# The ramp of a hybrid encoder layer: the w_ada sums of groups three and four at three places, with their block sums apart

## The chip, the cores and the metric

The kernel runs on one core of one Trainium2 chip. Its metric is the time of one execution in device microseconds (us). TensorE (PE in the profile) does the matrix products, VectorE (DVE) and ScalarE (ACT) the elementwise work, GpSimd (POOL) some memsets; the queue of SyncE (SP) issues nearly all DMA transfers. Each engine works through its own instructions in order and waits for others by semaphores.

## The reference, cut to what matters

```python
mod = jax.nn.silu(c) @ w_ada + b_ada                 # (1, 6144): shift, scale, gate
shift, scale, gate = jnp.split(mod, 3, axis=-1)
h = rmsnorm(x, pre_g) * (1.0 + scale[:, None]) + shift[:, None]
proj = h @ w_in                                      # (1024, 2048) @ (2048, 4608)
q, k, v, gate_a, u, gate_p = jnp.split(proj, SPLIT_POINTS, axis=-1)
y_a = windowed_gqa(q, k, v, rel_table, sink) * jax.nn.silu(gate_a)
y_p = multiscale_pool(u, w_pool_grp, pool_scale) * jax.nn.silu(gate_p)
g = jax.nn.sigmoid(h @ w_merge + b_merge)
g_a, g_p = jnp.split(g, N_BRANCHES, axis=-1)
merged = g_a * (y_a @ w_br_attn) + g_p * (y_p @ w_br_pool)
return x + gate[:, None] * rmsnorm(merged @ w_out, post_g)
```

Everything is float32; x is 1024 rows of 2048 columns. The change concerns only `silu(c) @ w_ada` for shift and scale, and the order in which weights arrive.

## The kernel before, in words

**Products.** The large products run by Strassen's scheme: seven products per 2 x 2 block step instead of eight, each on float32 values split into a high and a low part. `strassen` (L213) is a generator that yields after each of its seven products; `product` (L234) issues, for each, high x high, low x high and high x low. On PE a product's output bank is called X, V or Z. The seven in order are X (moving operand B11), V (T3), Z (T2), X again (B21), V again (T4), Z again (T1), and Z a last time (B22). `run` (L325) steps one generator for a pair of 128-column weight blocks; the seventh product of a run is put off (`late`) and issued by `flush` (L320) in the next run, after its second product.

For the weights, ACT writes the high part `whi` and DVE the low part `wlo` (both have four buffers) from the raw weights `raw` (four joint buffers), and DVE forms weight sums in `raw` and `ws`. After its second V product, DVE's addition `u<-V,u` empties bank V, and the next run's V product needs that bank.

**The ramp.** At the start, the normalized and modulated input h is not there yet; it is produced 512 columns at a time. w_ada's columns for shift and scale are taken in groups of 256 each. Group j of w_ada (16 tiles `ada`, one for each k block of 128 rows) gives the scale and shift for two k blocks of h. `modulation` (L476) makes four steps of four k blocks each: thin matmuls (GEMV, 32 columns wide, stationary operand `scz`, the silu of c) into one bank; after the fourth step ACT copies the bank to `acc`, `sum_columns` (L454) adds the four 32-row parts on PE (PM, the block sums), and `mod_columns` (L460) writes the columns `modc` on DVE. `fill` (L551) then modulates x, and makes the split operands B11 to B22 (the "op tiles") of one j with about a dozen instructions on each of ACT and DVE.

Groups one and two (j = 0, 1) are summed before the products. Five column pairs of w_in then run over the first half of k (j = 0, 1): pair one in plain blocks, pairs two to five as runs one to four of `ramp_gen` (L598). After these, the same five pairs run over the second half of k (j = 2, 3), which needs groups three and four. Their sums are issued between the products of runs one and two, by the table `late_sums` (L633): `run` calls one entry of `side` after each of its seven places, so entry 0 stands after run one's X, entry 6 after its last Z, entry 7 after run two's X; at a run's third place the put-off product of the run before is issued.

**What sets the order.** PE's order is that of the code; the instructions of `modulation` are pinned. ACT, DVE and SP are ordered by a scheduler from the same code, with pinned instructions (`keep`) in code order. On SP the w_ada tiles and raw weights are issued in the order of the code at L615 to L629; in the ramp SP has at most eight transfers under way, so a transfer is issued when an earlier one has landed. Raw weights of pair i are fetched by `fetch_raws` (L607); group four's tiles are ten in a pool of their own (`ada_tile`, L446) and six in slots of the large pool (`ada_slots`, L467).

Of the kernel before, what the change touches and what calls it, by code (L numbers as in the profile page):

```python
# [43 lines left out]
def encoder_layer(ctx: ExitStack, tc: tile.TileContext, x, c, table, w_ada, b_ada, pre_g,  # L44
# [32 lines left out]
    def uid(s):  # L77
        cnt[0] += 1
        return f"{s}_{cnt[0]}"

    def bank(tag, name="b"):
        return psum.tile([P, 512], F32, tag=tag, name=uid(name), bufs=1 if tag in SEEDED else 2)

    def slot(name, dt=F32R, shape=(P, 512)):
        return big.tile(list(shape), dt, tag="big", name=uid(name))

    def f32(ap):
        return ap.bitcast(F32)


    def keep(ins):

        tc.keep_in_program_order(ins)
# [31 lines left out]
    RAMP = 5  # L125
# [55 lines left out]
    def load_raws(w, n0, rows, js, pin=False):  # L181

        raws = []
        nj = len(js)
        joint = wp.tile([P, 2, nj, 256], F32, tag="raw", name=uid("raw"), bufs=4) if nj < 4 else None
        for kh in range(2):
            r = joint[:, kh] if nj < 4 else wp.tile([P, nj, 256], F32, tag="raw", name=uid("raw"), bufs=4)
            ins = load(r, rows(w, js, kh)[:, :, n0:n0 + 256])
            if pin:
                keep(ins)  # L190
            raws.append(r)
        return raws
# [6 lines left out]
    def rows_in_turn(part):  # L199

        def rows(w, js, kh):
            r0 = (part * 8 + 2 * js[0]) * P
            return w[r0:r0 + 2 * len(js) * P].rearrange("(k h p) n -> h p k n", h=2, p=P)[kh]
        return rows
# [135 lines left out]
    def weight_of(n0):  # L340
        return (w_in, n0) if n0 < NIN else (w_merge, n0 - NIN)
# [104 lines left out]
    def ada_tile(j, q):  # L446
        at = xa.tile([P, 2, 4, P], F32, tag="xa", name=uid("ada"))
        for kk in range(2):
            r0 = (2 * q + kk) * P
            keep(load(at[:, kk].rearrange("p (g h) n -> p g (h n)", g=2),  # L450
                      w_ada[r0:r0 + P, 0:2 * D].rearrange("p (g n) -> p g n", g=2)[:, :, j * 256:(j + 1) * 256]))
        return at

    def sum_columns(acc):  # L454
        pm = bank("at", "PM")
        for g in range(4):
            nc.tensor.matmul(pm[:, g:g + 1], acc[:, g, :], ones, start=True, stop=True)
        return pm

    def mod_columns(j, pm):  # L460
        tc.keep_in_program_order(nc.vector.tensor_tensor(
            modc[:, :, :, j], pm[:, 0:4].rearrange("p (g h) -> p g h", g=2),
            cols[:, 16:48].rearrange("p (g k) -> p g k", g=2)[:, :, 2 * j:2 * j + 2], ALU.add))
        keep(nc.vector.scalar_tensor_tensor(modc[:, 1, :, j], modc[:, 1, :, j], 1.0,
                                            cols[:, 48 + 2 * j:50 + 2 * j], op0=ALU.add, op1=ALU.mult))

    def ada_slots(j, kcs=range(KT)):  # L467
        tiles = []
        for kc in kcs:
            tiles.append(slot("ada", F32, (P, 4, P)))  # L470
            load(tiles[-1].rearrange("p (g h) n -> p g (h n)", g=2),
                 w_ada[kc * P:(kc + 1) * P, 0:2 * D].rearrange("p (g n) -> p g n", g=2)
                 [:, :, j * 256:(j + 1) * 256])
        return tiles

    def modulation(j, tile_of, pin=False):  # L476

        st_ = {}

        def step(q, between=None):  # L480
            if q == 0:
                st_["pv"] = bank("at", "GEMV")
            pv = st_["pv"]
            for kc in range(4 * q, 4 * q + 4):
                g = kc % 4 * 32
                ins = nc.tensor.matmul(pv[g:g + 32, :], scz[:, kc, :], tile_of(kc), start=kc < 4,
                                       stop=kc >= 12, tile_position=(0, g))
                if pin:
                    tc.keep_in_program_order(ins)
            if q == 3:  # L490
                acc = xa2.tile([P, 4, P], F32, tag="acc", name=uid("acc"), bufs=2)
                tc.keep_in_program_order(
                    nc.scalar.activation(acc, pv.rearrange("p (g n) -> p g n", g=4), AF.Copy))
                if between:
                    between()
                mod_columns(j, sum_columns(acc))

        return [partial(step, q) for q in range(4)]

    def weigh(acc, t, kc):  # L500

# [42 lines left out]
    def claim(j):  # L544

        for name in MOVING:
            op[name][j] = slot(f"{name}h"), slot(f"{name}l")
            for t in op[name][j]:
                nc.gpsimd.memset(f32(t)[:, 0:1], 0.0)
# [57 lines left out]
    def fetch_raws(i):  # L607
        raws.append(load_raws(*weight_of(ORDER[i]), rows_in_turn(0), [0, 1], True))
# [6 lines left out]
    ada = [ada_slots(0)]  # L615
# [7 lines left out]
    claim(0)  # L623
    ada.append(ada_slots(2))
    claim(1)
    ada3 = [ada_tile(3, q) for q in range(5)]
    ada3 = [at[:, kk] for at in ada3 for kk in range(2)] + ada_slots(3, range(10, KT))
    for i in range(3, RAMP):
        fetch_raws(i)  # L629

    group2 = deque(modulation(2, ada[2].__getitem__, True))
    group3 = modulation(3, ada3.__getitem__, True)
    late_sums = {1: [group2[0]], 3: list(group2)[1:3], 6: [group2[3], group3[0]], 9: group3[1:3], 12: group3[3:]}  # L633
    side = deque((lambda n=n: [step() for step in late_sums.get(n, ())]) for n in range(13))
    for s in range(2):
        for si in range(4 * s, 4 * s + 4):
# [32 lines left out]
    def take(queue, n):  # L669
        for _ in range(min(n, len(queue))):  # L670
            queue.popleft()()

    def hi_then_lo(blks, j):
        pieces = [plain_block(blk, j) for blk in blks]
        return deque(p for part in (slice(0, 4), slice(4, 6)) for block_ in pieces for p in block_[part])

    s0, s1, s2, s3 = modulation(0, ada[0].__getitem__, True)
    s0()
    s1()
    turns, put_by = turn_round(1, 1, (0, 1))  # L680
# [13 lines left out]
    take(turns, 5)  # L694
    right_top.append(fill_blocks(0))
    put_by()
    s0, s1, s2, s3 = modulation(1, ada[1].__getitem__, True)
    take(hi_then_lo(("11", "21"), 0), 12)
    s0()
    s1()  # L700
# [16 lines left out]
    def between(n):  # L717
        if n == 1:
            a11, a21 = (raws[1][0][:, :, nt * P:(nt + 1) * P] for nt in range(2))
            second["hi"], second["lo"] = ([wp.tile([P, 2, P], F32R, tag=t, name=uid(t), bufs=4) for _ in range(2)]  # L720
                                          for t in ("whi", "wlo"))
            split(second["hi"][0], second["lo"][0], a11, True)
            second["s3"] = wp.tile([P, 2, P], F32, tag="ws", name=uid("ws"))
            keep(sub(second["s3"], a11, a21))
        elif n == 3:
            split(second["hi"][1], second["lo"][1], second["s3"], True)
# [30 lines left out]
    i = RAMP  # L757
# [113 lines left out]
    for j in range(4, 8):  # L871
        sums_of, columns = ada_sums(j)
# [97 lines left out]
    with pool("attn") as ap:  # L970
# [27 lines left out]
        qraw, q, bt, g, pr, pv, opened = {}, {}, {}, {}, {}, {}, []  # L998
# [640 lines left out]
```

## Time and profile before

| what | before |
|---|---|
| median of 3 runs | 2118.74 us (2118.1 to 2118.84) |
| the profiled execution | 2117.89 us |
| its span in the profile | 2116.1 us |
| PE busy | 2083.9 us, 98% |
| DVE busy | 1541.3 us, 73% |
| ACT busy | 1106.8 us, 52% |
| PE waits from 66 to 98 us | 1.2 (V for u), 0.7 (PM for acc), 0.5 (V for T3h), 0.2 us (V for T3l) |

Of the rows below, those of the order of time give the start in us, the duration in us, the engine, the line of the kernel, the operation, output<-inputs by the program's names without buffer numbers, the shape, and how many were merged; in brackets stands the idle time of the engine before it and what ended it. A merged row's duration is from the first start to the last end; matmuls overlap in the pipeline, so the distance of two starts tells their cost. A sum over four k blocks shows as x8, a PM as x8, and half of one third of a product as x1. SPq is SP's queue issuing a transfer.

### The profile page before, as it was taken

The page shows a single profiled execution, that of the slowest core. Times are in us where ns is not written, and L with a number is a line of the kernel's source. Part 1 is how long each engine was busy: PE and PEld are TensorE (multiplying, and loading weights), DVE is VectorE, ACT ScalarE, POOL GpSimd, SP SyncE. Part 2 cuts the span into 40 slices and gives each one's busy share as a digit, 9 for nine tenths or more (in the row PEclk, how much of TensorE's full clock was granted, in tenths as well). Part 3 has the DMA queues.
Part 4 walks back from the last instruction along what each step waited for, and adds up shares of the span by engine and source line. Part 5 has one row for each costly group of instructions (what it writes and reads, how often), then busy time and mean ns, then how long its engine had stood idle before and what let it go on. Part 6 is the DMA issues. An engine that isn't in the chain of part 4 may idle for free.

```text
span 2116.1 us, 29011 instructions
## 1 busy us (share of the span) xinstructions
PE 2083.9 (98%) x9573; PEld 1715.0 (81%) x9573; DVE 1541.3 (73%) x2771; ACT 1106.8 (52%) x2106; POOL 20.1 (1%) x90
## 2 busy tenths in 40 slices
PE   6999999999999999999999999999999999999998
PEld 4688888888888888888888888888788788888887
DVE  5787667777546776677777677866957977879667
ACT  4654444443366544666655543333645644767554
POOL 0000000000000000000000000000000000000000
PEclk9999999999999999999999999999999999999999
DMA  9886666899767456544645476776755566686897
GB/s 330 278 268 226 205 192 208 292 306 324 255 194 238 149 177 203 171 158 158 197 149 163 156 230 216 219 233 197 237 173 160 184 193 194 220 316 217 294 321 249
DMA packets 302998, 468.20 MB, mean 221 GB/s; under 512 B 24138, under 2 KB 145122, under 8 KB 302848
## 3 DMA queue, kind: packets, MB, share of 16 engines
q1 hardware_dynamic: 299472, 457.82, 66.5%
q0 software_dynamic: 3040, 8.48, 1.0%
q8 instruction: 75, 1.23, 0.2%
q14 instruction: 75, 0.61, 0.1%
q10 hardware_dynamic: 336, 0.06, 0.0%
HBM read 341.45 MB, written 126.90 MB: 221 GB/s over the span
## 4 chain that ended last, share of the span: by engine, by line
PE 91%; DMA 5%; DVE 2%; ACT 1%; issue 1%; SPq 0%; DVEq 0%; POOL 0%; ACTq 0%; POOLq 0%
PE Z L238 31%; PE X L238 20%; PE V L238 20%; PE Z L1349 2%; PE Z L1351 2%; PE Z L1350 2%; DMA ada<-in_w_ada_dram 2%; DMA xt<-in_x_dram 1%; PE V L1351 1%; PE X L1351 1%; PE V L1349 1%; PE X L1349 1%; PE X L1350 1%; PE V L1350 1%; PE PT L1060 1%
## 5 line engine op out<-in xcount | busy, mean ns | idle before, releaser
L96 ACT ACTIVATE whi<-raw 128x512 fp32r<-128x512 f32 (+1 forms) x532 | 322.0, 606 | 508.8 <-PE Z L238 252.0
L97 DVE TENSOR_TENSOR wlo<-raw,whi 128x512 fp32r<-128x512 f32 (+1 forms) x532 | 347.8, 658 | 164.5 <-PE Z L238 122.7
L97 DVE TENSOR_TENSOR wlo<-wr,whi 128x512 fp32r<-128x512 f32 x224 | 150.6, 690 | 51.2 <-ACT whi L96 44.9
L96 ACT ACTIVATE whi<-wr 128x512 fp32r<-128x512 f32 x224 | 138.3, 629 | 86.0 <-DVE wlo L97 31.9
L103 DVE TENSOR_TENSOR raw<-raw,raw 128x512 f32<-128x512 f32 x79 | 54.6, 691 | 106.2 <-DMA raw<-in_w_merge_dram 82.0
L238 PE MATMUL V<-T3h,whi 128*128 128x512 f32 x334 | 91.4, 392 | 1.7 <-DVE u L103 1.2
L238 PE MATMUL Z<-T1h,whi 128*128 128x512 f32 x334 | 91.5, 392 | 0.9 <-ACT u L248 0.9
L238 PE MATMUL Z<-T2h,whi 128*128 128x512 f32 x334 | 91.2, 392 | 0.3 <-ACT whi L96 0.3
L238 PE MATMUL X<-B11h,whi 128*128 128x512 f32 x334 | 91.3, 391 | 0.0
L96 ACT ACTIVATE whi<-ws 128x512 fp32r<-128x512 f32 (+1 forms) x88 | 53.5, 608 | 72.0 <-PE X L238 63.9
L238 PE MATMUL Z<-B22h,whi 128*128 128x512 f32 x334 | 91.1, 392 | 0.0
L238 PE MATMUL V<-T4l,whi 128*128 128x512 f32 x334 | 90.7, 390 | 0.3 <-DVE T4l L97 0.2
L238 PE MATMUL X<-B21h,whi 128*128 128x512 f32 x334 | 90.8, 391 | 0.0
L238 PE MATMUL Z<-T2h,wlo 128*128 128x512 f32 x334 | 90.3, 390 | 0.5 <-DVE wlo L97 0.5
L238 PE MATMUL V<-T3l,whi 128*128 128x512 f32 x334 | 90.5, 390 | 0.2 <-DVE T3l L97 0.2
L238 PE MATMUL V<-T4h,whi 128*128 128x512 f32 x334 | 90.6, 391 | 0.0
L238 PE MATMUL Z<-T1l,whi 128*128 128x512 f32 x334 | 90.4, 390 | 0.1
L238 PE MATMUL X<-B11l,whi 128*128 128x512 f32 x334 | 90.4, 390 | 0.0
L238 PE MATMUL Z<-T1h,wlo 128*128 128x512 f32 x334 | 90.3, 390 | 0.0
L238 PE MATMUL X<-B11h,wlo 128*128 128x512 f32 x334 | 90.2, 390 | 0.0
L238 PE MATMUL Z<-B22l,whi 128*128 128x512 f32 x334 | 90.2, 390 | 0.0
L238 PE MATMUL X<-B21l,whi 128*128 128x512 f32 x334 | 90.2, 389 | 0.0
(358 smaller groups left out, 4840.4 us busy)
## 6 DMA issues: line engine op xcount, KB each, us to landing
part<-part_d SPq DMA_DIRECT2D x136, 256.0 KB, 5.1
ada<-in_w_ada_dram SPq DMA_DIRECT2D x128, 256.0 KB, 5.4
raw<-in_w_merge_dram SPq DMA_DIRECT2D x64, 512.0 KB, 5.8
raw<-in_w_in_dram SPq DMA_DIRECT2D x62, 512.0 KB, 4.2
wr<-ws_dS SPq DMA_DIRECT2D x60, 512.0 KB, 5.5
wr<-in_w_out_dram SPq DMA_DIRECT2D x48, 512.0 KB, 5.3
proj_d<-part SPq DMA_DIRECT2D x68, 256.0 KB, 2.2
sw<-in_w_out_dram SPq DMA_DIRECT2D x64, 256.0 KB, 6.1
```

Source lines behind the costliest of these rows:

```text
L96: ins = (nc.scalar.activation(hi, src, AF.Copy), nc.vector.tensor_tensor(lo, src, f32(hi), ALU.subtract))
L97: nc.vector.tensor_tensor(lo, src, f32(hi), ALU.subtract))
L103: return (eng or nc.vector).tensor_tensor(o, a, b, ALU.add)
L238: nc.tensor.matmul(ps, w_[:, i], op[mov][j][m_], start=fresh and i == 0 and n == 0, stop=i == nj - 1 and n == 2, skip_group_check=True)
L1060: nc.tensor.transpose(pt[:, i * P:(i + 1) * P], p[:, i * P:(i + 1) * P], ident)
L1349: nc.tensor.matmul(pb, hi, w[0], start=first, stop=False, skip_group_check=True)
L1350: nc.tensor.matmul(pb, lo, w[0], start=False, stop=False, skip_group_check=True)
L1351: nc.tensor.matmul(pb, hi, w[1], start=False, stop=last, skip_group_check=True)
```

## The change: what it does

The block sums are no longer part of `modulation`'s fourth step; they are a step of their own, `columns`, when `apart` is set. Groups three and four set it. The table then has the first four k blocks of group three after run one's X, the other twelve after its second X, and the block sums after its second V; all sixteen k blocks of group four after run two's first Z and its block sums after run two's second X. Before, they stood at entries 1, 3, 6, 9 and 12 in portions of four, eight, eight (four of each group), eight and four, with each group's block sums in its last portion. Groups one and two ignore the new step. Finally `fetch_raws(3)`, the raw weights of pair four, is called ahead of group four's tiles instead of behind them.

```diff
-    def modulation(j, tile_of, pin=False):
+    def modulation(j, tile_of, pin=False, apart=False):
...
                 if between:
                     between()
-                mod_columns(j, sum_columns(acc))
-
-        return [partial(step, q) for q in range(4)]
+                st_["acc"] = acc
+                if not apart:
+                    columns()
+
+        def columns():
+            mod_columns(j, sum_columns(st_["acc"]))
+
+        return [partial(step, q) for q in range(4)] + [columns]
...
     claim(1)
+    fetch_raws(3)
     ada3 = [ada_tile(3, q) for q in range(5)]
     ada3 = [at[:, kk] for at in ada3 for kk in range(2)] + ada_slots(3, range(10, KT))
-    for i in range(3, RAMP):
+    for i in range(4, RAMP):
         fetch_raws(i)
 
-    group2 = deque(modulation(2, ada[2].__getitem__, True))
-    group3 = modulation(3, ada3.__getitem__, True)
-    late_sums = {1: [group2[0]], 3: list(group2)[1:3], 6: [group2[3], group3[0]], 9: group3[1:3], 12: group3[3:]}
+    group2 = modulation(2, ada[2].__getitem__, True, True)
+    group3 = modulation(3, ada3.__getitem__, True, True)
+    late_sums = {0: group2[:1], 4: group2[1:4], 5: group2[4:], 10: group3[:4], 11: group3[4:]}
...
-    s0, s1, s2, s3 = modulation(0, ada[0].__getitem__, True)
+    s0, s1, s2, s3, _ = modulation(0, ada[0].__getitem__, True)
...
-    s0, s1, s2, s3 = modulation(1, ada[1].__getitem__, True)
+    s0, s1, s2, s3, _ = modulation(1, ada[1].__getitem__, True)
```

PE, run one, between its first X and its first V (the piece of the difference; V's operands T3 are the last op tiles of the first half that DVE and ACT make). The names carry the program's tile numbers.

```order
 L238 MATMUL X_825<-B11h_360,wlo_755 128x512
+L486 MATMUL GEMV_835<-ada_328,scz 32x512
+L486 MATMUL GEMV_835<-ada_330,scz 32x512
+L486 MATMUL GEMV_835<-ada_332,scz 32x512
+L486 MATMUL GEMV_835<-ada_334,scz 32x512
 L238 MATMUL V_827<-T3h_304,whi_754 128x512
 L238 MATMUL V_827<-T3h_364,whi_754 128x512
```

Group three's first four k blocks, which stood behind V, stand ahead of it.

PE at group three's block sums, before: they stand in the middle of run two's X, with group four's first sums behind them.

```order
L238 MATMUL X_928<-B11l_361,whi_931 128x512
L457 MATMUL PM_916<-ones,acc_914 128x1 x4
L486 MATMUL GEMV_923<-ada_388,scz 32x512 x2
L486 MATMUL GEMV_923<-ada_391,scz 32x512 x2
L238 MATMUL X_928<-B11h_300,wlo_932 128x512
```

And now, in run one, between V and Z:

```order
L238 MATMUL V_827<-T4h_316,wlo_891 128x512
L238 MATMUL V_827<-T4h_376,wlo_891 128x512
L457 MATMUL PM_902<-ones,acc_888 128x1 x4
L238 MATMUL Z_826<-T1h_320,whi_909 128x512
L238 MATMUL Z_826<-T1h_380,whi_909 128x512
```

The block sums moved up by more than a product, and between the last sum and them lies a whole V product.

DVE around the addition that empties bank V in run one, before (`raw_415` are the raw weights of pair four):

```order
L97 TENSOR_TENSOR wlo_945<-ws_942,whi_944 128x256
L106 TENSOR_TENSOR ws_1058<-raw_415 128x256
L103 TENSOR_TENSOR raw_415<-raw_415 128x2x128
L103 TENSOR_TENSOR u_226_860<-V_827,u_226_860 128x512
L97 TENSOR_TENSOR wlo_957<-raw_294,whi_956 128x256
L97 TENSOR_TENSOR wlo_980<-raw_297,whi_979 128x256
L103 TENSOR_TENSOR p_222_841<-p_222_841,u_234_906 128x512
L461 TENSOR_TENSOR modc<-PM_916,cols 128x4
```

And now (`raw_388` are the same weights):

```order
L97 TENSOR_TENSOR wlo_940<-ws_937,whi_939 128x256
L106 TENSOR_TENSOR ws_1058<-raw_388 128x256
L103 TENSOR_TENSOR raw_388<-raw_388 128x2x128
L103 TENSOR_TENSOR u_226_860<-V_827,u_226_860 128x512
L461 TENSOR_TENSOR modc<-PM_902,cols 128x4
L97 TENSOR_TENSOR wlo_952<-raw_294,whi_951 128x256
L464 SCALAR_TENSOR_TENSOR modc<-modc,cols 128x2
```

The addition keeps its place behind the two instructions on pair four's raw weights; the modulation columns come directly behind it.

SP, before: pair four's raw weights (`raw_415`) behind the last tile of group four.

```order
L665 DMA ramp_d_86<-c_781 128x512
L471 DMA ada_413<-in_w_ada_dram 128x2x256
L188 DMA raw_415<-in_w_in_dram 128x2x256 x2
L188 DMA raw_418<-in_w_in_dram 128x2x256 x2
L665 DMA ramp_d_86<-c_786 128x512
```

And now (`raw_388`), between groups three and four:

```order
L471 DMA ada_356<-in_w_ada_dram 128x2x256
L471 DMA ada_358<-in_w_ada_dram 128x2x256
L188 DMA raw_388<-in_w_in_dram 128x2x256 x2
L450 DMA ada_391<-in_w_ada_dram 128x2x256 x2
L450 DMA ada_394<-in_w_ada_dram 128x2x256 x2
```

The two transfers passed the sixteen of group four, which all go out two places later; pair five's raw weights (`raw_418`) now go ahead of all four stores of pair one's results (`ramp_d`).

## The prediction

> **What bounds the kernel now.** I read the page's busy times and chain first, then a table of stretches, then the stage that the change touches, engine by engine.
>
> ```profile
> span 2116.1 us, 29011 instructions
> PE 2083.9 (98%) x9573; PEld 1715.0 (81%) x9573; DVE 1541.3 (73%) x2771; ACT 1106.8 (52%) x2106; POOL 20.1 (1%) x90
> PE 91%; DMA 5%; DVE 2%; ACT 1%; issue 1%; SPq 0%; DVEq 0%; POOL 0%; ACTq 0%; POOLq 0%
> ```
>
> PE is busy for 98% of the span and carries 91% of the chain. A change is therefore worth what it takes out of PE's own time or of PE's few gaps. The stretches (columns: span, then PE, PEld, DVE, ACT, POOL busy, granted clock, DMA share, GB/s) show where the gaps are:
>
> ```profile
> 22.00:29.00 7.00, 5.02 (x22) 4.75 (x23) 5.79 (x23) 4.04 (x14) 0.10 (x1) 0.53 1.06 377
> 29.00:36.00 7.00, 6.12 (x29) 2.21 (x29) 1.97 (x6) 1.38 (x3) 0.95 (x11) 0.99 1.10 348
> 36.00:42.00 6.00, 6.00 (x49) 4.08 (x50) 1.38 (x2) 1.19 (x2) 0.24 (x3) 1.00 1.10 346
> 66.00:98.00 32.00, 29.39 (x159) 17.08 (x158) 22.20 (x48) 19.20 (x40) 0.00 (x0) 1.00 0.83 277
> 98.00:117.00 19.00, 19.00 (x85) 15.74 (x84) 18.27 (x42) 16.10 (x34) 0.00 (x0) 1.00 0.63 204
> 117.00:170.00 53.00, 53.00 (x235) 43.71 (x234) 44.52 (x91) 27.22 (x56) 0.10 (x1) 1.00 0.84 278
> 170.00:400.00 230.00, 229.86 (x1029) 190.09 (x1028) 153.84 (x238) 94.82 (x154) 0.00 (x0) 1.00 0.67 212
> ```
>
> The moved sums lie between 66 and 98 us, runs one and two of the ramp. There PE is idle for 32.00 - 29.39 = 2.6 us; from 98 to 400 us it is idle for 0.14 us. What this stage loses or wins goes straight to the end, as long as no other engine or transfer falls behind.
>
> PE's order of time in that stage (start, duration, what, idle before it and its releaser):
>
> ```profile
> 66.03 0.63 PE L238 MATMUL X<-B11h,whi 128*128 128x512 f32 x2
> ...
> 67.40 0.39 PE L238 MATMUL V<-T3h,whi 128*128 128x512 f32 x1
> 68.23 0.50 PE L238 MATMUL V<-T3h,whi 128*128 128x512 f32 x1 [0.45 <-ACT T3h L96]
> ...
> 69.18 0.50 PE L238 MATMUL V<-T3l,whi 128*128 128x512 f32 x1 [0.22 <-DVE T3l L97]
> 69.52 0.63 PE L238 MATMUL V<-T3h,wlo 128*128 128x512 f32 x2
> 70.08 1.06 PE L486 MATMUL GEMV<-ada,scz 128*32 128x512 f32 x8
> 71.08 0.74 PE L238 MATMUL Z<-T2h,whi 128*128 128x512 f32 x2
> 71.66 0.63 PE L238 MATMUL Z<-T2l,whi 128*128 128x512 f32 x2
> ...
> 72.68 1.92 PE L486 MATMUL GEMV<-ada,scz 128*32 128x512 f32 x16
> 74.53 0.74 PE L238 MATMUL X<-B21h,whi 128*128 128x512 f32 x2
> ...
> 78.83 1.06 PE L486 MATMUL GEMV<-ada,scz 128*32 128x512 f32 x8
> ...
> 80.40 0.63 PE L238 MATMUL X<-B11l,whi 128*128 128x512 f32 x2
> 80.86 0.95 PE L457 MATMUL PM<-ones,acc 128*128 128x1 f32 x8
> ...
> 84.71 0.73 PE L238 MATMUL V<-T3h,whi 128*128 128x512 f32 x2 [1.24 <-DVE u L103]
> ...
> 96.75 1.05 PE L457 MATMUL PM<-ones,acc 128*128 128x1 f32 x8 [0.70 <-ACT acc L493]
> 97.66 0.71 PE L238 MATMUL Z<-T1h,wlo 128*128 128x512 f32 x2
> 98.21 0.62 PE L238 MATMUL X<-B11h,whi 128*128 128x512 f32 x2
> ...
> 107.74 0.62 PE L238 MATMUL X<-B11h,whi 128*128 128x512 f32 x2
> ```
>
> The reader should see four waits, 0.45 + 0.22 + 1.24 + 0.70 = 2.61 us, and the places where the stream of products is broken by sums (GEMV) or block sums (PM). Behind the 1.24 us stands DVE:
>
> ```profile
> 68.43 0.70 DVE L97 TENSOR_TENSOR T3l<-xT,T3h 128x512 fp32r<-128x512 f32 x1
> ...
> 82.92 0.43 DVE L106 TENSOR_TENSOR ws<-raw 128x256 f32<-128x256 f32 x1 [6.20 <-DMA raw<-in_w_in_dram]
> ...
> 83.97 0.68 DVE L103 TENSOR_TENSOR u<-V,u 128x512 f32<-128x512 f32 x1
> ```
>
> DVE stands for 6.20 us at the head of its queue on the raw weights of pair four, and the addition that empties bank V waits behind them. PE's next V waits for that addition.
>
> **The change, part by part.** I rebuild the stage from 66.03 us, the first product of run one, to the first product of run three, which stands at 98.21: 32.18 us, thirteen products and everything between them.
>
> *Products.* Their number stays. Seven of them without a break go from 98.21 to 107.74, 1.361 us each, 0.454 for a pair. Thirteen make 17.7 us, so the interruptions cost 32.18 - 17.7 = 14.5 us now.
>
> *Sums.* All 32 k blocks stay. Four blocks (x8) take 71.08 - 70.08 = 1.00 us, eight (x16) 74.53 - 72.68 = 1.85, so four more in the same place cost 0.85. A place adds a lead of 0.10 (69.52 + 0.454 to 70.08) and a slow first pair behind it, 71.66 - 71.08 = 0.58 instead of 0.454, so 0.12. Six places now become three: four blocks 1.22, twelve 2.70 + 0.22 = 2.92, sixteen 3.55 + 0.22 = 3.77 us. I extend the measured step to twelve and sixteen blocks, since two sizes are shown. If each further four cost a whole place's 1.22 again (the dear end), the two large places would cost 3.66 and 4.88, 1.8 us more; nothing between 72.68 and 74.53 speaks for it.
>
> *Block sums.* Each PM takes 97.66 - 96.75 = 0.91, no lead (80.40 + 0.454 to 80.86), and 98.21 - 97.66 = 0.55 for the pair after it, 0.10 more: 1.01 us, twice, 2.02. A product now lies between the last sum and the PM. ACT's copy of the sum, which PM reads, is thereby covered:
>
> ```profile
> 67.55 0.63 ACT L96 ACTIVATE T3h<-xT 128x512 fp32r<-128x512 f32 x1 [0.86 <-DVE xT L106]
> ...
> 80.05 0.60 ACT L493 ACTIVATE acc<-GEMV 128x512 f32<-128x512 f32 x1 [0.51 <-PE GEMV L486]
> ```
>
> It begins 0.16 us after the sums (78.83 + 1.06 = 79.89) and takes 0.60; a product is 1.36. The cover leaves 0.6 us. If ACT is late by more, PM waits again, as it does for 0.70 us now.
>
> *First sums ahead of V.* At 67.40 PE now goes into four blocks until about 68.5, where it would have waited for T3h and T3l. ACT's T3h ends at 68.18, DVE's T3l at 69.13. V restarts at 68.50 and its fourth matmul, which needs T3l, comes at 69.3. Both waits vanish, the second by only 0.1 us; V ends where it ends now, with the sums already done.
>
> *Raw weights of pair four.* SP's queue (issue, duration, what), and the time from issue to landing of the w_ada transfers between 62 and 100 us:
>
> ```profile
> 52.93 11.06 SPq L471 DMA_DIRECT2D ada<-in_w_ada_dram  x16
> 64.33 7.14 SPq L450 DMA_DIRECT2D ada<-in_w_ada_dram  x10
> 71.92 3.37 SPq L471 DMA_DIRECT2D ada<-in_w_ada_dram  x5
> ...
> 76.42 0.37 SPq L471 DMA_DIRECT2D ada<-in_w_ada_dram  x1
> 77.14 2.61 SPq L188 DMA_DIRECT2D raw<-in_w_in_dram  x4
> DMA to landing us min/median/max: 5.6/6.0/6.0
> ```
>
> The two raw transfers go from 77.14 to the place at 64.33. They took 82.92 - 77.14 = 5.8 us to land, so both are there by about 71, before DVE asks. The u addition then runs right behind the V product that ends near 77.0, and run two's V (about 80.7) finds its bank free: 1.24 us gone. Group four's sixteen w_ada transfers move back by two: from 64.33 to 76.42 the queue made sixteen steps, one of them a store, of 0.76 us each; the last tile now stands seventeen steps behind 64.33, so it goes out near 77.2 and lands near 83.2. The sums that need them now stand at about 84.9 to 88.5, the last tile at 88. Group three's last tile, out by 64.0, lands by 70; its sums are needed from 72.8 on. Pair five's raw weights keep their place in time, ahead now of four ramp stores, whose landing nobody on PE waits for soon.
>
> *The sum.* New interruptions: 1.22 + 2.92 + 3.77 + 2.02 = 9.9 us against 14.5. Gain 4.5 us, of which 2.6 are the four waits and the rest fewer starts and restarts. Run three begins near 93.7 instead of 98.2. From there on the order on PE is the old one. DVE is the engine to watch: 18.27 of 19.00 us between 98 and 117. Its work of both stretches, 22.20 + 18.27 = 40.5 us, now has 46.5 us, and the PMs that open the two fills come about 4 and 7 us earlier (77.0 for 80.86, 90.0 for 96.75), so I cost the fills at nothing. Were that cover gone, PE would wait for the operands of the second half, which is a rival below.
>
> The profiled execution took 2117.89 us (span 2116.1), 0.85 below the median of 2118.74. 2118.74 - 4.5 = 2114.2.
>
> **A rule weighed.** The longest stretch without full-width products grows from about 1.9 to 3.6 us. Early on PE does such narrow sums too:
>
> ```profile
> 32.61 3.31 PE L486 MATMUL GEMV<-ada,scz 128*32 128x512 f32 x8 [0.30 <-DMA ada<-in_w_ada_dram]
> ```
>
> The clock was 0.53 from 22 to 29 us, behind idle PE, but 0.99 and 1.00 around and after these thin sums. So I price the clock at nothing. [...]
>
> **Rivals.**
> - *A wait comes back.* ACT or DVE, with fills and splits in another order, is late for a PM or a V by as much as today: one PM 0.8 with its restart, both 1.6, a V 1.3 more. Gain 1.6 to 3.7: 2115.0 to 2117.1. For it: covers of 0.1 and 0.6 us. Against: DVE and ACT are busy 22.20 and 19.20 of 32 us here.
> - *The gain is not carried.* Fills or transfers, not PE, set the start of the second half: about 2118.7. For it: DVE at 96% between 98 and 117. Against: fills that start earlier.
> - *The clock falls.* A stretch like that at 22 us, 7.00 at 0.53, costs 7.00 x 0.47 = 3.3: 2117.5. Against: the clock after 32.61.
> - *Slower: group four's last tile.* Its sums stand in one block on PE's queue with everything behind them, where three places spread them before. If the last w_ada tile landed after 88 + 4.5 = 92.5 instead of 83, the gain would be gone; at 97 the kernel would be 4.5 us slower, 2123. For it: six of these tiles wait for slots that PE, DVE or ACT must free. Against: before, they went out by 76.42.
> - That the change doesn't do what it says is excluded by the order of instructions.
>
> **How the numbers follow.** About 0.2%, 4.2 us, is what a measurement of this kernel tells from no change; the forecast lies just beyond it. Forecast 0.78 (2113.6 to 2114.9; 0.10 of it lies within the 0.2%), a wait back 0.11, not carried 0.04, clock 0.03, slower 0.04. Faster: 0.78 - 0.10 = 0.68. Same: 0.10 + 0.11 + 0.04 + 0.03 = 0.28. Slower 0.04. The range takes the forecast, widened below by 0.6 for the spread of the runs (2118.1 to 2118.84) and above to the middle of the returned waits, 2116.6.
>
> **What would show it.** Three GEMV groups of 8, 24 and 32 on PE; no idle entry on V for u, T3h or T3l, and none on PM for acc; DVE's wait for raw weights gone from the time before u; run three's first X near 93.7, the second half's first near 112.8; PE full from there on. I am wrong if PE shows a new wait between 66 and 117 us, if a GEMV waits for w_ada, if the clock drops after the long sums, or if the 4.5 us are there at 94 us and gone at 170.

## The result and the profile after

| what | before | changed |
|---|---|---|
| median | 2118.76 us (10 runs, 2118.1 to 2121.4) | 2114.22 us (10 runs, 2112.54 to 2116.39) |
| the profiled execution (span) | 2117.89 us (2116.1) | 2115.21 us (2113.4) |
| run one's first X to run three's first X | 32.18 us | 27.50 us |
| run one's first X to the second half's first X | 51.24 us | 46.54 us |

The ratio of the changed kernel to before is 0.9976, with a 95% interval of 0.9967 to 0.9986: faster by 0.24%, 3.0 to 7.0 us. The predicted time was 2114.2.

The page of the changed kernel, its span and busy times:

```profile
span 2113.4 us, 29024 instructions
PE 2081.4 (98%) x9573; PEld 1715.9 (81%) x9573; DVE 1543.3 (73%) x2771; ACT 1108.2 (52%) x2106; POOL 20.2 (1%) x90
```

The same table of stretches as before (span, then PE, PEld, DVE, ACT, POOL busy, granted clock, DMA share, GB/s):

```profile
66.00:98.00 32.00, 32.00 (x179) 21.60 (x178) 27.32 (x61) 23.72 (x52) 0.00 (x0) 1.00 0.93 306
98.00:117.00 19.00, 19.00 (x85) 15.76 (x84) 16.46 (x36) 14.24 (x30) 0.00 (x0) 1.00 0.68 219
```

PE has no gap left between 66 and 98 us, where it had 2.6 us. DVE, which had 18.27 of 19.00 us between 98 and 117, now has 16.46; more of its work falls into the first stretch. PE's order of time:

```profile
66.19 0.62 PE L238 MATMUL X<-B11h,whi 128*128 128x512 f32 x2
...
67.65 1.07 PE L486 MATMUL GEMV<-ada,scz 128*32 128x512 f32 x8
68.65 0.73 PE L238 MATMUL V<-T3h,whi 128*128 128x512 f32 x2
...
72.97 2.78 PE L486 MATMUL GEMV<-ada,scz 128*32 128x512 f32 x24
75.68 0.72 PE L238 MATMUL V<-T4h,whi 128*128 128x512 f32 x2
...
77.17 0.95 PE L457 MATMUL PM<-ones,acc 128*128 128x1 f32 x8
77.98 0.71 PE L238 MATMUL Z<-T1h,whi 128*128 128x512 f32 x2
...
80.79 0.62 PE L238 MATMUL V<-T3h,whi 128*128 128x512 f32 x2
...
84.96 3.64 PE L486 MATMUL GEMV<-ada,scz 128*32 128x512 f32 x32
88.53 0.73 PE L238 MATMUL X<-B21h,whi 128*128 128x512 f32 x2
...
90.02 0.95 PE L457 MATMUL PM<-ones,acc 128*128 128x1 f32 x8
90.83 0.72 PE L238 MATMUL V<-T4h,whi 128*128 128x512 f32 x2
...
93.69 0.62 PE L238 MATMUL X<-B11h,whi 128*128 128x512 f32 x2
...
112.73 0.62 PE L238 MATMUL X<-B11h,whi 128*128 128x512 f32 x2
```

Three groups of sums and two of block sums, and no brackets: none of these rows waited. DVE, around the addition that empties bank V:

```profile
74.24 0.42 DVE L106 TENSOR_TENSOR ws<-raw 128x256 f32<-128x256 f32 x1
...
77.37 0.69 DVE L103 TENSOR_TENSOR u<-V,u 128x512 f32<-128x512 f32 x1 [2.24 <-PE V L238]
```

The 6.20 us on the raw weights of pair four are gone; the addition now waits for its product, as it should. SP's queue shows why, with the raw weights ahead of group four's tiles:

```profile
64.15 1.12 SPq L188 DMA_DIRECT2D raw<-in_w_in_dram  x2
65.66 7.14 SPq L450 DMA_DIRECT2D ada<-in_w_ada_dram  x10
73.24 4.12 SPq L471 DMA_DIRECT2D ada<-in_w_ada_dram  x6
```

In this one profile only 2.7 of the 4.7 us reach the end of the span. PE's waits of more than 0.15 us behind 115 us sum to 5.07 us in it and to 3.15 in that of before. Over the fourteen kernels profiled in this study that sum goes from 2.1 to 6.1 us, in no order with what the ramp does, and single runs of one kernel scatter by 3 to 8 us. That these waits make the scatter is likely but not shown, since each kernel has one trace. The ten runs of each kernel average over it: 4.5 us between the medians. Below I therefore read each experiment from run one's first X to the second half's first X, which is 46.54 us in the change, and give the medians beside it. This also leaves out that run one's first X itself comes at 65.6 to 67.3 us in the fourteen traces, a difference that is there before 47 us, ahead of everything that the edits touch on PE.

### The profile page after: what moved, and what is told of

Its sections match the earlier page's. It is cut to its first block, busy times and chain, and to the rows that moved or that the text cites. A ratio compares the mean times of both kernels' runs of the same rounds, so it can differ in the third digit from the quotient of the medians.

```text
span 2113.4 us, 29024 instructions
## 1 busy us (share of the span) xinstructions
PE 2081.4 (98%) x9573; PEld 1715.9 (81%) x9573; DVE 1543.3 (73%) x2771; ACT 1108.2 (52%) x2106; POOL 20.2 (1%) x90
## 4 chain that ended last, share of the span: by engine, by line
PE 89%; DVE 4%; DMA 3%; issue 1%; SPq 0%; ACT 0%; DVEq 0%; ACTq 0%
PE Z L238 30%; PE V L238 20%; PE X L238 20%; PE Z L1355 2%; PE Z L1357 2%; PE Z L1356 2%; PE V L1355 1%; PE V L1357 1%; PE V L1356 1%; DMA raw<-in_w_merge_dram 1%; PE X L1355 1%; PE X L1356 1%; PE X L1357 1%; PE PT L1066 1%; DVE wlo L97 1%
## 5 line engine op out<-in xcount | busy, mean ns | idle before, releaser
L238 PE MATMUL V<-T3h,wlo 128*128 128x512 f32 x334 | 90.2, 389 | 0.0
```

Of the source, the lines that this page charges most:

```text
L238: nc.tensor.matmul(ps, w_[:, i], op[mov][j][m_], start=fresh and i == 0 and n == 0, stop=i == nj - 1 and n == 2, skip_group_check=True)
```

## The experiments

| kernel | first X to second half, us | against the change | median, us (runs) | ratio to before, 95% |
|---|---|---|---|---|
| raw weights alone | 48.84 | +2.30 | 2116.86 (11) | 0.9991 (0.9982 to 1.0) |
| table alone | 52.25 | +5.71 | 2120.38 (11) | 1.0003 (0.9994 to 1.0012) |
| block sums joined | 49.97 | +3.43 | 2117.17 (11) | 0.9988 (0.9979 to 0.9997) |
| first sums behind V | 47.75 | +1.21 | 2116.41 (11) | 0.9988 (0.9979 to 0.9997) |
| eight places | 48.48 | +1.94 | 2114.85 (11) | 0.9982 (0.9973 to 0.999) |
| block sums put off | 49.21 | +2.67 | 2116.17 (11) | 0.9987 (0.9978 to 0.9996) |
| group four split, joined | 47.51 | +0.97 | 2115.34 (11) | 0.9982 (0.9973 to 0.999) |
| group three at once | 46.58 | +0.04 | 2115.05 (11) | 0.9982 (0.9973 to 0.9991) |
| raws behind 12, 13, 14 tiles | 47.43, 48.27, 50.65 | +0.89, +1.73, +4.11 | 2116.17, 2120.2, 2122.02 (1 each) | |
| idle behind thin sums | 48.95 | +2.41 | 2116.78 (1) | |

### Raw weights alone

```diff
--- before
+++ raw weights alone
     claim(1)
+    fetch_raws(3)
     ada3 = [ada_tile(3, q) for q in range(5)]
...
-    for i in range(3, RAMP):
+    for i in range(4, RAMP):
```

> The kernel before, with pair four's raw weights ahead of group four, nothing else. By the prediction's terms DVE no longer stands for them, V's wait of 1.24 us and its restart of 0.12 go: the second half's first X comes at 115.9 us instead of 117.3, the time falls by 1.4 us (0.07%). The three other waits stay. Rival: the earlier raw weights are worth nothing by themselves, another wait takes the place of V's: 117.3 us, no change.

It gained 2.40 us, not 1.4. V's wait for u is gone, and so is the 0.70 us that group four's block sums waited for acc; the two waits are 1.94 of the 2.40, and stops and restarts around them the rest. ACT in before, and then ACT and PE here:

```profile
95.27 0.63 ACT L96 ACTIVATE B22h<-xT 128x512 fp32r<-128x512 f32 x1
95.80 0.41 ACT L96 ACTIVATE whi<-raw 128x256 fp32r<-128x256 f32 x1
96.10 0.59 ACT L493 ACTIVATE acc<-GEMV 128x512 f32<-128x512 f32 x1
```

```profile
92.50 0.62 ACT L96 ACTIVATE B22h<-xT 128x512 fp32r<-128x512 f32 x1
93.03 0.41 ACT L96 ACTIVATE whi<-raw 128x256 fp32r<-128x256 f32 x1
94.17 0.60 ACT L493 ACTIVATE acc<-GEMV 128x512 f32<-128x512 f32 x1 [0.74 <-PE GEMV L486]
94.99 0.95 PE L457 MATMUL PM<-ones,acc 128*128 128x1 f32 x8
```

Before, acc stood in ACT's queue behind the last instructions of group three's fill. With the raw weights early the fill ends 2.8 us sooner, and ACT itself waits for the sums. So the 0.70 us was an echo of DVE's stand at the raw weights. It was not the missing product between sums and block sums, which is missing here too.

### Table alone

```diff
--- changed kernel
+++ table alone
     claim(1)
-    fetch_raws(3)
     ada3 = [ada_tile(3, q) for q in range(5)]
...
-    for i in range(4, RAMP):
+    for i in range(3, RAMP):
```

> The change without the move of pair four's raw weights: they stay behind group four's tiles and land near 83 us. If the two parts are independent, the table alone is worth 4.5 - 1.4 = 3.1 us: the second half's first X at 114.2 us. If the raw weights' landing is what V really waits for, PE only arrives earlier at the same wait: V of run two, due at 80.7 us, starts near 84.7, a wait of about 4 us, and of the 4.5 us about 0.5 is left: X at 116.8 us.

V's wait came as expected, but the second half began later still. DVE, PE, and then a stretch:

```profile
83.03 0.42 DVE L106 TENSOR_TENSOR ws<-raw 128x256 f32<-128x256 f32 x1 [8.80 <-DMA raw<-in_w_in_dram]
84.78 0.73 PE L238 MATMUL V<-T3h,whi 128*128 128x512 f32 x2 [3.82 <-DVE u L103]
```

```profile
85.30:88.70 3.40, 3.40 (x9) 2.60 (x9) 3.40 (x8) 3.40 (x7) 0.00 (x0) 0.51 0.96 329
```

The table brings run two's first V earlier, while the raw weights land when SP's queue lets them: what is saved ahead becomes a longer wait. Then the granted clock halves for 3.4 us, which costs some 1.7 more. So the parts don't add: -2.40 by the raw weights alone, +1.01 by the table alone (-0.7 without the half clock, by estimate), -4.70 together.

### Block sums joined to the last sums

```diff
--- changed kernel
+++ block sums joined
-    late_sums = {0: group2[:1], 4: group2[1:4], 5: group2[4:], 10: group3[:4], 11: group3[4:]}
+    late_sums = {0: group2[:1], 4: group2[1:], 10: group3}
```

> The change, but each group's block sums called in the same place as its last sums. They then stand four or five matmuls later in PE's order, 0.9 to 1.1 us, instead of a whole product of 1.36 us. ACT's copy needs 0.16 + 0.60 us. By the prediction's cover no wait comes back as long as ACT is free: second half's first X at 112.7 us, as in the change, within 0.2. Rival: the product in between is what removed PM's wait: 0.7 to 0.8 us come back for each, X at 114.2 us.

Group three's block sums waited for nothing. Group four's did, and dearly; ACT and PE, then the stretch behind:

```profile
85.80 0.60 ACT L310 ACTIVATE c<-Z 128x512 f32<-128x512 f32 x1 [2.56 <-PE GEMV L486]
...
89.98 0.61 ACT L96 ACTIVATE B22h<-xT 128x512 fp32r<-128x512 f32 x1
90.50 0.57 ACT L493 ACTIVATE acc<-GEMV 128x512 f32<-128x512 f32 x1
91.13 1.05 PE L457 MATMUL PM<-ones,acc 128*128 128x1 f32 x8 [1.59 <-ACT acc L493]
```

```profile
92.40:95.80 3.40, 3.40 (x10) 2.66 (x9) 2.23 (x6) 2.74 (x5) 0.00 (x0) 0.52 0.22 80
```

The sums had ended at 88.11; ACT came to acc 2.4 us later, behind the fill of group three, and the wait of 1.59 us has 1.7 us of half clock behind it. The missing product made at most a small part of it. ACT in the change:

```profile
88.97 0.59 ACT L493 ACTIVATE acc<-GEMV 128x512 f32<-128x512 f32 x1
89.44 0.63 ACT L96 ACTIVATE B22h<-xT 128x512 fp32r<-128x512 f32 x1
```

Counted from run one's first X, the sums end at 22.34 us in both kernels, and the block sums could have started at 23.77 here and did start at 23.83 in the change. But acc begins at 24.73 here and at 22.78 in the change. Two things differ on ACT. The scheduler put acc behind B22h here and ahead of it in the change. And ACT stood for 2.56 us at `c<-Z`, where the change stands for 1.12 (at 85.09). In both kernels `c<-Z` starts 0.08 to 0.09 us after the first store of pair one's results (`ramp_d<-c`) has landed, at 85.72 here and at 85.00 in the change; the GEMV that the row names had ended earlier. So this run shows what a late copy costs. What the product in between is worth by itself, with ACT in one order, no run shows.

### First sums behind V

```diff
--- changed kernel
+++ first sums behind V
-    late_sums = {0: group2[:1], 4: group2[1:4], 5: group2[4:], 10: group3[:4], 11: group3[4:]}
+    late_sums = {1: group2[:1], 4: group2[1:4], 5: group2[4:], 10: group3[:4], 11: group3[4:]}
```

> The change, but group three's first four k blocks behind run one's V, where they were. By the prediction the waits for T3h and T3l return, 0.45 + 0.22 us and two restarts, 1.2 us between V's start and its end in all: second half's first X at 113.9 us instead of 112.7. Rival: the sums ahead of V cost as much as they hide, since V is late for its operands either way: 112.7 us.

PE's two waits are back, with their restarts, 1.21 us in all:

```profile
69.40 0.50 PE L238 MATMUL V<-T3h,whi 128*128 128x512 f32 x1 [0.45 <-ACT T3h L96]
...
70.34 0.50 PE L238 MATMUL V<-T3l,whi 128*128 128x512 f32 x1 [0.21 <-DVE T3l L97]
```

### Eight places

```diff
--- changed kernel
+++ eight places
-    late_sums = {0: group2[:1], 4: group2[1:4], 5: group2[4:], 10: group3[:4], 11: group3[4:]}
+    late_sums = {0: group2[:1], 1: group2[1:2], 3: group2[2:3], 4: group2[3:4], 5: group2[4:], 7: group3[:1], 8: group3[1:2], 9: group3[2:3], 10: group3[3:4], 11: group3[4:]}
```

> The changed kernel with its 32 sums in eight places of four k blocks instead of three; block sums as in the change. Theory (a place costs a fixed 0.37 us: 1.22 for four blocks less 0.85 for four more): five more places, 1.85 us. From run one's first X to the second half's first X it was 46.54 us in the changed kernel; here 48.4. Rival (what costs is the block, not the place; the gain of 4.5 us was the waits and the earlier fill alone): 46.5 to 46.8. Second rival (the thin blocks of 24 and 32 drew on something that short ones spare, so that shorter blocks gain): below 46.5.

Five more places cost 1.94 us, 0.39 each. No row waits; only starts and restarts were added. The time of its runs, 2114.85, cannot tell it from the change.

### Group three's block sums put off

```diff
--- changed kernel
+++ block sums put off
-    late_sums = {0: group2[:1], 4: group2[1:4], 5: group2[4:], 10: group3[:4], 11: group3[4:]}
+    late_sums = {0: group2[:1], 4: group2[1:4], 10: group2[4:] + group3[:4], 11: group3[4:]}
```

> The changed kernel with group three's block sums put off to the end of group four's sums, 8 to 9 us later. PE issues the same instructions. Theory (DVE and ACT have cover for the fills): no wait on PE but small ones; the block sums save a restart of about 0.1, so 46.3 to 46.6 us from run one's first X to the second half's first X, as in the change (46.54). Rival (the fill's start sets the second half; the change gained by starting the fill early, which freed ACT and DVE): group three's fill then falls together with group four's, ACT is late for group four's acc or the second half waits for its operands B11 to B22: 2 us or more later, 48.5 or above, with a named wait on PE for acc, B or u.

The rival holds: group three's block sums now stand at 84.13 us, ACT begins the fill at 87.54 and is late for acc. PE, and two stretches cut at the steps of its clock:

```profile
91.16 1.05 PE L457 MATMUL PM<-ones,acc 128*128 128x1 f32 x8 [0.93 <-ACT acc L493]
```

```profile
88.86:92.28 3.42, 2.49 (x15) 1.89 (x15) 3.38 (x7) 3.12 (x8) 0.00 (x0) 1.00 0.48 176
92.28:95.69 3.41, 3.41 (x9) 2.63 (x9) 1.98 (x7) 2.26 (x5) 0.00 (x0) 0.50 0.21 77
```

Behind a wait of 0.93 us the granted clock was 0.50 here; behind 1.24 us (before, V for u) it had stayed at 1.00.

### Group four's sums split, block sums joined

```diff
--- changed kernel
+++ group four split, joined
-    late_sums = {0: group2[:1], 4: group2[1:4], 5: group2[4:], 10: group3[:4], 11: group3[4:]}
+    late_sums = {0: group2[:1], 4: group2[1:4], 5: group2[4:], 9: group3[:2], 10: group3[2:]}
```

> The changed kernel with group four's sums in two places of eight k blocks and its block sums joined to the last. The run with joined block sums showed 1.59 us of idle PE behind a stretch of 3.64 us of thin sums, and then 3.4 us of products at half the clock. Here the same idle stands behind 1.9 us of thin sums. Theory one (idleness alone drops the clock): the wait of about 1.6 and the window at 0.5 both come: 46.5 + 0.4 for the place + 1.6 + 1.6 = 50.1 us from run one's first X to the second half's. Theory two (thin sums and idleness together drop it): the wait comes and the clock stays near 1.0: 48.5. If ACT is early enough, the wait shrinks to 0.6 and below, 47.5, and the run says nothing of the clock.

The last case came: the block sums waited 0.30 us, the clock stayed, 47.51 us. The extra place makes the sums end only 0.4 us later than in the run with joined block sums (22.74 us from run one's first X, for 22.34). The larger part is ACT's: acc begins 1.1 us earlier (23.61 for 24.73), and stands ahead of B22h again, as in the change.

### Group three at once

```diff
--- changed kernel
+++ group three at once
-    late_sums = {0: group2[:1], 4: group2[1:4], 5: group2[4:], 10: group3[:4], 11: group3[4:]}
+    late_sums = {0: group2[:4], 3: group2[4:], 10: group3[:4], 11: group3[4:]}
```

> The changed kernel with all sixteen sums of group three at one place, behind run one's first X, and the block sums behind its first Z, so two places instead of three. Theory (a place costs 0.37 us, and group three's tiles are landed by 70): 46.54 - 0.37 = 46.2 us from run one's first X to the second half's, with group three's fill 2 to 3 us earlier; in the whole time below what its runs can tell. Rival (the last w_ada tile of group three is late, or the put-off V comes behind what ACT and DVE then do): a wait on the sums for a tile, or on V for u, of 0.3 to 2 us: 46.5 to 48.5.

46.58 us: one place less, and yet nothing gained. PE's block sums and what stands on ACT ahead of the copy that they read:

```profile
85.89 0.60 ACT L310 ACTIVATE c<-Z 128x512 f32<-128x512 f32 x1 [2.11 <-DMA ramp_d<-c]
...
89.25 0.62 ACT L96 ACTIVATE B22h<-xT 128x512 fp32r<-128x512 f32 x1
89.77 0.59 ACT L493 ACTIVATE acc<-GEMV 128x512 f32<-128x512 f32 x1
...
90.41 1.05 PE L457 MATMUL PM<-ones,acc 128*128 128x1 f32 x8
```

The last X pair ahead of them starts at 89.67, so they could start at 90.12; acc makes them 0.29 late, and behind a stop they take 0.91 instead of 0.81, which together makes 0.39, as much as the 0.37 that was to be saved. The cover of group four's block sums is thin, and the earlier fill didn't widen it: ACT stood for 2.11 us until the first store of pair one's results had landed, and then had acc behind B22h, not ahead of it as in the change. Neither was tried without the other. No kernel of the study has a shorter ramp or a lower median than the change, but the intervals of all except the table alone overlap with its own.

### Raw weights behind twelve, thirteen and fourteen tiles

These three, and the next, ask when a wait halves the clock. Here V waits among ordinary products, for longer with each tile.

```diff
--- changed kernel
+++ raws behind 12 (13, 14)
-    fetch_raws(3)
     ada3 = [ada_tile(3, q) for q in range(5)]
-    ada3 = [at[:, kk] for at in ada3 for kk in range(2)] + ada_slots(3, range(10, KT))
+    ada3 = [at[:, kk] for at in ada3 for kk in range(2)] + ada_slots(3, range(10, 12))
+    fetch_raws(3); ada3 += ada_slots(3, range(12, KT))
```

> The changed kernel with the raw weights of pair four behind twelve of group four's sixteen tiles. With all sixteen ahead V waited 3.82 us for u; each tile takes 0.7 us of SP's queue, so the wait should be 3.82 - 4 x 0.7 = 1.0 us, with ordinary products ahead of it and no thin sums. Theory one (any idle time of about a microsecond may drop the clock): after the wait the products stand at twice their distance for some 3.4 us, 46.54 + 1.0 + 0.1 + 1.7 = 49.3 us from run one's first X to the second half's. Theory two (thin sums count as little work, and the 0.93 and 1.59 us of idleness dropped the clock only because 3.6 us of thin sums or block sums stood around them): the clock stays at 1.0, 47.7 us.

> The changed kernel with the raw weights of pair four behind thirteen of group four's sixteen tiles. V should wait 3.82 - 3 x 0.7 = 1.7 us for u, as long as the 1.59 us that dropped the clock behind the thin sums of 24 and 32, but among ordinary products. Theory one (idleness alone): clock near 0.5 for 3.4 us after it, 46.54 + 1.7 + 0.1 + 1.7 = 50.0 us from run one's first X to the second half's. Theory two (thin sums count too): clock at 1.0, 48.4 us.

> The changed kernel with the raw weights of pair four behind fourteen of group four's sixteen tiles. V should wait 3.82 - 2 x 0.7 = 2.4 us for u among ordinary products, between the 1.24 us that left the clock alone before and the 3.82 us that dropped it. Theory one (idleness alone, any over about one microsecond): clock near 0.5 after it, 46.54 + 2.4 + 0.1 + 1.7 = 50.7 us from run one's first X to the second half's. [...]

With twelve, V started 0.3 us late and showed no wait of its own; the Z behind it was another 0.3 us late, for ACT's u, here and with thirteen. With thirteen the clock stayed at 1.00 in the window of V's wait and in the next, with fourteen it fell (for each kernel V's row, then the stretch with its wait, and for fourteen the next one):

```profile
82.08 0.73 PE L238 MATMUL V<-T3h,whi 128*128 128x512 f32 x2 [0.97 <-DVE u L103]
```

```profile
81.45:84.86 3.41, 2.63 (x10) 1.89 (x11) 3.37 (x9) 2.33 (x5) 0.00 (x0) 1.00 1.07 385
```

```profile
84.22 0.73 PE L238 MATMUL V<-T3h,whi 128*128 128x512 f32 x2 [2.14 <-DVE u L103]
```

```profile
81.82:85.23 3.41, 1.27 (x6) 0.86 (x5) 2.48 (x8) 0.55 (x1) 0.00 (x0) 1.00 1.08 369
85.23:88.65 3.42, 3.42 (x9) 2.47 (x8) 3.42 (x8) 3.42 (x8) 0.00 (x0) 0.50 1.06 351
```

Theory two holds with twelve and thirteen tiles, theory one with fourteen. The waits were 0.3 to 0.7 us shorter than expected. The single time with thirteen, 2120.2, has another cause beside the ramp: V waited 3.56 us for u at 1437 us, and the clock was 0.50 for 6.83 us behind it.

### Idle behind thin sums

```diff
--- raws behind 13
+++ idle behind thin sums
-    late_sums = {0: group2[:1], 4: group2[1:4], 5: group2[4:], 10: group3[:4], 11: group3[4:]}
+    late_sums = {0: group2[:1], 7: group2[1:4], 9: group2[4:], 10: group3[:4], 11: group3[4:]}
```

> The changed kernel with the raw weights of pair four behind thirteen of group four's sixteen tiles, as in the run where V waited 0.97 us among ordinary products and the clock stayed at 1.0, but with group three's twelve last sums (24 thin matmuls, about 2.8 us) put from ahead of run one's second V to right ahead of the waiting V, and its block sums behind them. V still waits for u until about 82.1, now some 1.1 us behind 2.8 us of thin sums, with no block sums between. Theory one (thin sums of 512 columns count as little work, so idleness behind them drops the clock): V and the products after it stand at 0.85 us a pair for some 3.4 us, granted clock near 0.5 from 82 to 86. Theory two (thin sums count as work; what counted as idle in the joined run and in the one with the block sums put off was the wait and the block sums of one column together, 0.93 + 0.9 and 1.59 + 0.9 us): the clock stays at 1.0 from 82 to 86 and pairs at 0.455 us.

V waited 2.27 us, twice what I expected, since the block sums had left the stretch ahead of it too. And the clock stayed up; V's row, and the stretches:

```profile
82.28 0.73 PE L238 MATMUL V<-T3h,whi 128*128 128x512 f32 x2 [2.27 <-DVE u L103]
```

```profile
77.14:80.56 3.42, 2.86 (x25) 0.68 (x24) 0.12 (x1) 1.18 (x3) 0.00 (x0) 1.00 1.11 348
80.56:83.97 3.41, 1.69 (x7) 1.42 (x8) 3.05 (x8) 0.60 (x3) 0.00 (x0) 1.00 1.09 368
83.97:87.38 3.41, 3.41 (x20) 2.77 (x18) 2.27 (x7) 2.43 (x4) 0.00 (x0) 1.00 1.06 381
```

Theory one, that thin sums count as little work, falls: the stretch from 77.14 holds almost nothing but 24 thin matmuls. But length alone doesn't decide either, since 2.14 us dropped the clock and 2.27 did not. What does stands in the last section.

## Why the prediction was right

**The total.** That the median meets 2114.2 to 0.02 us is in part luck: the interval of the difference is 3.0 to 7.0 us, and in the profiled execution 2.7 us reach the end. The ramp is the better witness, 4.7 us against 4.5. The runs make it up from three parts: 2.40 by the raw weights alone, 1.21 by the first sums ahead of V, and 1.1 to 1.2 by three places fewer at 0.37 to 0.39, in all 4.7 to 4.8. (The upper end of the range, 2116.6, is said to be the middle of 2115.0 and 2117.1; that is 2116.05. Nothing hangs on it.)

**Places and sums** were right to 0.02 us. From the rows above, with a lead of 0.09 to 0.10: four blocks 1.20 (foretold 1.22), twelve 2.91 (2.92), sixteen 3.78 (3.77). That the step of 0.85 per four blocks extends to sixteen, which two sizes only suggested, holds; and eight places gave 0.39 for a place, where the sum had 0.37.

**Block sums** cost 77.98 - 77.17 = 0.81 and a restart of 0.09, 0.90 each instead of 1.01. This is the largest error of the sum, 0.2 us: the 0.91 I took came from a group that had waited. All interruptions make 27.50 - 17.7 = 9.8 us (foretold 9.9), of which these rows account for 9.7, and seven products from 93.69 to 103.21 make 1.360 each (1.361).

**First sums ahead of V** removed both waits, as expected by the step, and putting them back cost 1.21 us.

**Raw weights.** The addition started at 77.37 (77.0), the last tile of group four went out at 77.0 (77.2), its sums began at 84.96 (84.9). Nothing waited for a tile, so the rival of the late tile was far off. But the attribution was too simple: the sum gave V's wait to the raw weights and PM's wait to the separation. The raw weights alone remove both, and without them the rest of the change makes the ramp 1.0 us longer, of which the half clock is 1.7. The total is right because both are in the change; of the 4.7 us next to nothing is left for the separation of sums and block sums.

**The stores.** The prediction let pair five's raw weights pass four stores, "whose landing nobody on PE waits for soon". The first of them went out at 79.25 us instead of 75.62 and landed at 85.0. Not PE but ACT waits for it, at `c<-Z`: for 1.12 us in the change, where it cost PE nothing, and for 1.7 to 2.7 us in four of the other kernels (block sums joined or put off, group four split, group three at once). In each of the four PE's block sums then came to wait for acc; how much of that is the store's was not taken apart.

**The cover of block sums.** The prediction gave 0.6 us. In the change ACT copied group four's acc from 88.97 to 89.56, and the block sums started at 90.02: 0.46 us. The edits that moved the fill or joined the block sums used that up, each with another order on ACT. The rival "a wait comes back" priced such a wait at 0.8 with its restart. Measured, it was 0.3 in one kernel, and 0.93 and 1.59 us with 1.7 us of half clock on top in two: that price was too low, by the clock and in one of them by the wait itself. The change has acc ahead of B22h; the two kernels with an earlier fill (block sums joined, group three at once) have it behind, and an earlier fill with the change's order was not tried.

**Not carried.** Run three began at 93.69 (93.7), the second half at 112.73 (112.8). DVE had cover, because both fills came earlier; where group three's fill was made late, ACT did not.

**The clock.** It was priced at nothing for a stretch of 3.6 us of thin sums, and it stayed at 1.00. In the change the clock does not fall between 33 us and the last 5 us of the span. The rival's price of 3.3 us was about twice too high for one fall: where one came in the ramp, it held 3.41 us at 0.50, 1.7 us. And PE was not idle ahead of the stretch at 22 us from which that price was taken: in the window before it, 18.96 to 22.37, it was busy for 1.60 of 3.41 us. What the prediction called idle is half worked, which is the subject of the last section.

## What to carry to other kernels

Read a wait together with what its releaser was doing: DVE's stand at one late load cost 1.24 us at a V, and, through a later fill, 0.70 us more at block sums 12 us on. Fetch what stands at the head of such an engine's queue before rearranging anything else, since an earlier consumer only waits longer for a load that hasn't moved. And where a tiny matmul reads another engine's copy, look at what that engine has to do first, its waits for stores included: block sums waited when ACT came late, whatever PE did in between, and 1.59 us of waiting cost 3.3 with the clock.

## What the runs showed of the hardware

What had not been expected is what halves the clock in the middle of a busy stage. In the granted clock of each trace, its steps lie on a grid of 3.413 us: with the block sums put off they fall at 24.01, 30.84 and 92.28 us, 2 and 18 steps apart. I therefore cut PE's time of all fourteen kernels, from 40 us to the end, at that kernel's own grid, and summed in each window the time with a product or a thin sum of 512 columns under way, without the block sums of one column.

| kernel | window, us | products and thin sums, us of 3.41 | clock in the next window |
|---|---|---|---|
| table alone | 81.98 to 85.39 | 0.60 | 0.50 |
| raws behind 13 | 1433.13 to 1436.54 | 0.85 | 0.50 |
| block sums joined | 88.82 to 92.23 | 0.91 | 0.50 |
| raws behind 14 | 81.82 to 85.23 | 1.27 | 0.50 |
| block sums put off | 88.86 to 92.28 | 1.57 (2.49 with block sums) | 0.50 |
| idle behind thin sums | 80.56 to 83.97 | 1.69 | 1.00 |
| before | 94.05 to 97.46 | 2.00 (2.71 with block sums) | 1.00 |
| first sums behind V | 637.66 to 641.07 | 2.04 | 1.00 |

These are the windows with the least work. After each of the five below 1.6 us the clock fell, after none of the others, and there was no other fall until the last microseconds of the span. It stayed at 0.50 for one window after four of them and for two after the fifth. So in these runs, from 40 us on, the clock fell behind a window of 3.41 us that was worked for up to 1.57 us, and stayed at 1.00 behind those of 1.69 us and more: the border is at about half. Thin sums count as work here (the change has a window of 3.41 us with 0.48 us of full-width products and no fall); block sums of one column do not, or the window with 2.49 us would have stood where that with 1.69 did. The wait of 2.27 us lay across a border of the grid, 0.56 us in one window and 1.72 in the next, and by this table that is why it was harmless and 2.14 us were not. Among these windows the border lies between 1.57 and 1.69 us, as far as PE's modelled ends can tell; one kernel stands close on each side of it, and no run was made to narrow it.

The start of the kernel puts it a little higher. From the first step that a trace tells (17 to 21 us) to 34 us, PE turns x by matmuls of 128 columns (`XT`), with many short pauses. There, 21 windows at full clock had up to 1.71 us of work, and the clock fell after every one; the least work without a fall is 1.96 us (group four split, 28.19 to 31.60). The window with 1.71 us, in the change, and the next:

```profile
26.52:29.94 3.42, 1.71 (x13) 1.33 (x12) 2.35 (x11) 1.68 (x6) 0.29 (x3) 1.00 1.09 359
29.94:33.35 3.41, 3.05 (x16) 2.16 (x17) 1.75 (x4) 1.19 (x2) 0.10 (x1) 0.50 1.10 347
```

Its longest pause is 0.91 us, so it is the sum over a window that counts and not the longest pause; the table alone could not tell the two apart. Over all windows the border is near half, somewhere from 1.57 to 1.96 us, and perhaps not the same for matmuls of 128 and of 512 columns.

The grid lies differently in the traces: the first fall stands at 22.37 us before, 23.11 in the change, 23.97 with the block sums joined. That a fall behind a wait of one or two microseconds therefore belongs to the profiled execution, and that another run of the same kernel may go without it, is an inference and not shown, since each kernel has one trace. A wait of 3.82 us leaves at least 1.91 us without work in one window, so at most 1.50 us of work, wherever the border of the grid lies; by this table (an estimate) it should drop the clock each time.
